# An encoder layer on one core: the output projection and the gate as plain products with pre-split A sides

## The chip, the core and the metric

One core of a Trainium2 chip runs the whole program once. The engines are TensorE (PE, with its weight loads as PEld), VectorE (DVE), ScalarE (ACT), GpSimd (POOL) and SyncE (SP), which issues the transfers between DRAM and SBUF. The metric is the device time of one execution in microseconds, from the first to the last instruction and what lies around that; lower is better.

## What is computed

A hybrid encoder layer on two sequences of 1024 tokens of width 1024, a prompt and a sample, in float32. The part that the change touches, cut from the reference:

```python
att = attention_mixer(q, k, v, rel_bias)
ssm = ssm_mixer(u, ..., w_glu, b_glu)
mix = jnp.concatenate([rms_norm(att, g_att_out), rms_norm(ssm, g_ssm_out)], axis=-1)
h = h + mix @ w_out
f = rms_norm(h, g_mlp)
h = h + jnp.square(jax.nn.relu(f @ w_mlp1)) @ w_mlp2
e = rms_norm(h, g_ple)
h = h + jax.nn.sigmoid(e @ w_ple_gate) * (p_i @ w_ple_proj)
return rms_norm(h, g_final)
```

`w_out` and `w_ple_gate` are 1024x1024, `w_mlp1` is 1024x4096, `w_ple_proj` 256x1024. The mixers' outputs `att` and `ssm` are 512 wide each.

## The kernel before

**Split precision.** Every float32 operand of a matmul is split into a high part (`hi`, a cast on ACT, L1145) and a low part (`lo`, the operand less `hi`, on DVE or POOL, L1146). `mm3` multiplies hi by hi, lo by hi and hi by lo into one PSUM bank, so one product step is three matmuls, at L451, L452 and L453. A matmul here has a 128x128 stationary side and a 128x512 moving side.

**Three phases.** Phase A norms the input, projects q, k, v and u and runs the state-space mixer. Phase B runs the dilated attention of both sequences, with the GLU of the mixer (`Glu`, its norm at L1035) and the norm of the attention's output (`att_norm`) woven in. Its order is written by hand: tasks of generators that name the engine and the place at which they go on. Phase C (`PhaseC.run`) goes through the sequences one after the other: `mix @ w_out` into `h`, the MLP in 8 chunks of 512 hidden columns, the gate, the final norm. In phase C the program text is put in order by a scheduler that simulates a timeline; each engine then works in that fixed order, and so does SP with its transfers.

**The mixers' outputs.** `Glu` (sequence by sequence) and `att_norm` (prompt in phase B) or `AttNorm` (sample, one token tile or two per chunk of the prompt's MLP) store transposed float32 tiles in the DRAM scratch `ssm` and `mixa`. Phase C loads them as `mix0mixa`, `mix0ssm` (tokens 0 to 511, L1210) and `mix1mixa`, `mix1ssm` (512 to 1023).

**The products.** `product` multiplies A (features x tokens) and B (weights, a half of 512 columns) over k steps of 128. In each step it splits A's 128x512 piece on ACT and DVE and B's on ACT and POOL, from the pool `ops` with three buffers of each kind, and issues 12 matmuls into four PSUM banks of the pool `pm2` (five banks). `strassen` forms a 2x2 block product from seven such block products. For `w_out` and the gate a block product has four k steps, 48 matmuls. Its sums of blocks are operations of 128x1024 or 128x2048 on DVE and POOL (L1174 to L1185), before which the next block product cannot be split. `into_h` and, in the gate, `read` add the banks into `u2`, `h`, `g2`, `g22` and `pre`. The MLP's second product uses `strassen` in chunks 0 to 6 and plain `product` in chunk 7.

**Around them.** The norm of `h` (`norm`, one call for each half of four token tiles) takes squares on ACT, a Newton iteration on DVE, a scaling (`ft`, L524), transposes on PE (`n_ps`, L529) and `put`: for the MLP into `Act`, high and low part; for the gate into `Blocks`, float32, split later in `product`. In the gate `pj` is `p @ w_ple_proj` for one token tile and half, 6 matmuls into a bank of `pm1` (three banks), and `sg` (L1381, L1382, from the pool `raw` with three tiles) the sigmoid and its product with `pj`.

## Time and profile before

| | us |
|---|---|
| median of 3 runs | 2838.79 |
| fastest and slowest of them | 2838.08, 2844.15 |
| the profiled execution | 2836.98 |
| its span, first to last instruction | 2835.2 |
| PE busy | 2583.4 (91%), 12014 matmuls |
| DVE busy | 1888.1 (67%) |
| ACT, POOL busy | 1177.9, 1231.5 |

The profile is of one execution; the times of single instructions are from it. Matmuls overlap in the engine, so the mean duration of one (about 0.4 us) is longer than the distance between two that follow each other. "Idle before" in a row is time in which the engine stood still ahead of those instructions, and the name behind the arrow is what ended it.

### The profile page before, as it was taken

What the parts mean: (1) busy time and instruction counts of PE and PEld (TensorE: products, weight loads), DVE (VectorE), ACT (ScalarE), POOL (GpSimd) and SP (SyncE); (2) the same over time, 40 slices, a digit from 0 to 9 for tenths busy, and PEclk for the clock granted to TensorE, in tenths of its full rate; (3) what the DMA queues carried; (4) which work ended last, traced back from release to release, by engine and by line L of the source; (5) the groups of instructions that cost most, each with busy time, mean ns of one, the idle gap of its engine ahead of it and who ended that gap; (6) DMA issues with size and microseconds to landing.
All of it is one profiled execution on the core that took longest, in us unless ns stands there. A gap on an engine that the chain in (4) does not pass through costs nothing.

```text
span 2835.2 us, 33802 instructions
## 1 busy us (share of the span) xinstructions
PE 2583.4 (91%) x12014; PEld 2036.4 (72%) x12014; DVE 1888.1 (67%) x3075; ACT 1177.9 (42%) x2370; POOL 1231.5 (43%) x845
## 2 busy tenths in 40 slices
PE   6998888969998789999999998968899999999986
PEld 5766766755566567888888776746788888888765
DVE  7867786566777784555765638799555555447677
ACT  5323323336568244333333335434433333333534
POOL 2122333223322553544645536565444555545554
PEclk9989988989999899999999999989999999999998
DMA  9524543354444401211221022142011111111201
GB/s 326 130 56 120 163 155 105 94 172 141 125 144 158 160 30 41 67 53 56 67 64 52 23 90 71 53 155 101 30 53 52 45 41 56 60 56 43 84 8 60
DMA packets 252264, 252.46 MB, mean 89 GB/s; under 512 B 41136, under 2 KB 208048, under 8 KB 250048
## 3 DMA queue, kind: packets, MB, share of 16 engines
q1 hardware_dynamic: 251072, 250.18, 27.8%
q8 instruction: 94, 1.54, 0.2%
q14 instruction: 74, 0.61, 0.1%
q0 software_dynamic: 1024, 0.13, 0.0%
HBM read 188.76 MB, written 59.27 MB: 87 GB/s over the span
## 4 chain that ended last, share of the span: by engine, by line
PE 66%; DVE 24%; issue 4%; DMA 3%; ACT 3%; POOL 1%; SPq 0%; DVEq 0%; ACTq 0%; POOLq 0%
PE m L452 16%; PE m L451 16%; PE m L453 16%; DVE lo L1146 3%; DVE h L1231 2%; PE ag L453 2%; PE glu L992 2%; PE ag L451 2%; PE ag L452 2%; PE pss L761 1%; PE po L822 1%; PE pt L801 1%; PE n_ps L529 1%; PE s_pb L251 1%; DVE s_br L358 1%
## 5 line engine op out<-in xcount | busy, mean ns | idle before, releaser
L452 PE MATMUL m<-hi,lo 128*128 128x512 f32 x1360 | 535.7, 403 | 61.4 <-DVE lo L1146 60.8
L1146 POOL TENSOR_TENSOR lo<-wr_b,hi 128x512 fp32r<-128x512 f32 x228 | 334.1, 1475 | 512.3 <-ACT hi L1145 487.3
L453 PE MATMUL m<-lo,hi 128*128 128x512 f32 x1360 | 528.3, 400 | 1.1 <-POOL lo L1146 1.0
L451 PE MATMUL m<-hi 128*128 128x512 f32 x1360 | 499.6, 402 | 19.6 <-DVE h L1231 8.6
L1231 DVE TENSOR_TENSOR h<-h,m 128x512 f32<-128x512 f32 x512 | 326.6, 678 | 139.8 <-PE m L453 139.8
L451 PE MATMUL m<-acth,hi 128*128 128x512 f32 x1024 | 400.2, 392 | 5.1 <-DVE actl L447 4.1
L453 PE MATMUL m<-actl,hi 128*128 128x512 f32 x1024 | 400.1, 391 | 3.6 <-DVE actl L447 3.6
L452 PE MATMUL m<-acth,lo 128*128 128x512 f32 x1024 | 400.1, 391 | 0.0
L452 PEld LDWEIGHTS m<-hi,lo 128*128 128x128 f32 x1360 | 262.7, 194 | 131.4 <-DVE lo L1146 76.1
L451 PEld LDWEIGHTS m<-hi 128*128 128x128 f32 x1360 | 260.9, 193 | 82.1 <-DVE h L1231 13.6
L453 PEld LDWEIGHTS m<-lo,hi 128*128 128x128 f32 x1360 | 262.9, 193 | 58.9 <-POOL lo L1146 2.4
L1145 ACT CAST hi<-wr_b 128x512 fp32r<-128x512 f32 x228 | 141.4, 621 | 377.6 <-PE m L452 339.7
L1146 DVE TENSOR_TENSOR lo<-hid,hi 128x512 fp32r<-128x512 f32 x200 | 183.6, 920 | 160.9 <-ACT hi L1145 160.9
L1146 POOL TENSOR_TENSOR lo<-w,hi 128x512 fp32r<-128x512 f32 x128 | 178.1, 1399 | 149.3 <-ACT hi L1145 136.5
L451 PEld LDWEIGHTS m<-acth,hi 128*128 128x128 f32 x1024 | 192.2, 188 | 49.1 <-ACT acth L446 5.1
L453 PEld LDWEIGHTS m<-actl,hi 128*128 128x128 f32 x1024 | 192.6, 188 | 46.2 <-DVE actl L447 4.9
L452 PEld LDWEIGHTS m<-acth,lo 128*128 128x128 f32 x1024 | 192.7, 188 | 41.2
L1293 ACT ACTIVATE hid<-m 128x512 f32<-128x512 f32 x128 | 76.1, 595 | 222.5 <-PE m L453 222.4
L453 PE MATMUL ag<-actl,whi 128*128 128x512 f32 x384 | 153.1, 400 | 0.0
L451 PE MATMUL ag<-acth,whi 128*128 128x512 f32 x384 | 152.8, 398 | 0.0
L452 PE MATMUL ag<-acth,wlo 128*128 128x512 f32 x384 | 152.6, 397 | 0.0
L1145 ACT CAST hi<-hid 128x512 fp32r<-128x512 f32 x200 | 123.3, 618 | 33.7 <-DVE hid L1181 32.1
(382 smaller groups left out, 4692.5 us busy)
## 6 DMA issues: line engine op xcount, KB each, us to landing
w<-in_w_mlp_dram SPq DMA_DIRECT2D x128, 256.0 KB, 2.8
wr_b<-in_w_mlp_dram SPq DMA_DIRECT2D x32, 1024.0 KB, 4.9
wraw<-in_w_in_dram SPq DMA_DIRECT2D x32, 512.0 KB, 4.4
out_dram<-h SPq DMA_DIRECT2D x16, 512.0 KB, 2.7
v<-zv SPq DMA_DIRECT2D x8, 576.0 KB, 6.5
xt<-in_x_sample_dram SPq DMA_DIRECT2D x8, 512.0 KB, 8.1
xt<-in_x_prompt_dram SPq DMA_DIRECT2D x8, 512.0 KB, 5.9
act_scr<-acth SPq DMA_DIRECT2D x4, 1024.0 KB, 7.3
```

The source lines that it names most:

```text
L251: nc.tensor.matmul(pb[:, k], w[:, i, g + k], u[:, g + k], start=True, stop=True)
L358: v.tensor_tensor(q4(sre), q4(sre), S_, op=ALU.mult)
L451: nc.tensor.matmul(out, l[0], r[0], start=first, stop=False)
L452: nc.tensor.matmul(out, l[1], r[0], start=False, stop=False)
L453: nc.tensor.matmul(out, l[0], r[1], start=False, stop=last)
L529: nc.tensor.transpose(pt[:, i], dst[:, P * k:P * k + P], ident)
L761: self.nc.tensor.matmul(pss[h][:, u, w], ql, kr, start=True, stop=True)
L992: nc.tensor.matmul(o, self.w[:, k, P * f:P * f + P], gt[k][:, c], start=k == 0, stop=k == 3)
L1145: self.nc.scalar.copy(hi, src)
L1146: lo_eng.tensor_tensor(lo, src, hi.bitcast(F32), op=ALU.subtract)
L1231: eng.tensor_tensor(o, o, x, op=ALU.add)
L1293: nc.scalar.activation(z, o, AF.Relu)
```

## The change

The products of `w_out` and of the gate are no longer made by `strassen` but as four plain calls of `product`, one for each half of the tokens and half of the columns, over all eight k steps: 96 matmuls each. `product` takes an `Act` as its A side and then splits only B. The A sides come split: `Glu`, `att_norm` and `AttNorm` make the high and low part and store both, in scratch of twice the size (the diff shows `att_norm`; `AttNorm.put` does the same with two tiles of its pool), and the gate's norm writes into an `Act` in place of `Blocks`, which is gone. `mixed` loads the parts into an `Act`. The pool of activation tiles is two pools of four, one for each half of the tokens; the first is opened at the end of phase B. The weights of one use are four tiles of 1 MB (`square`) in the tags of the hidden layer's and the MLP weights' tiles; `w_ple_proj`'s parts move to other tags. All adds of the gate into `h` are on DVE. The final norm goes over pairs of token tiles.

```diff
@@ class Glu
             v.scalar_tensor_tensor(go[f], go[f], self.cols[:, 4 + f:5 + f], rows, op0=ALU.mult, op1=ALU.mult)
-            nc.sync.dma_start(out=self.scr["ssm", s][f, :, 512 * th:512 * th + 512], in_=go[f])
+            hi, lo = (self.two.tile([P, 512], F32R, tag="g" + x, name="g" + x) for x in "hl")
+            nc.scalar.copy(hi, go[f])
+            nc.gpsimd.tensor_tensor(lo, go[f], hi.bitcast(F32), op=ALU.subtract)
+            for i, x in enumerate((hi, lo)):
+                nc.sync.dma_start(out=self.scr["ssm", s][i, f, :, 512 * th:512 * th + 512], in_=x.bitcast(F32))
...
@@ def att_norm
-        o = pool.tile([P, 4, P], F32, tag="ao", name="ato", bufs=2)
-        nc.scalar.copy(o, px)
+        hi, lo = (pool.tile([P, 4, P], F32R, tag="a" + x, name="ato", bufs=n) for x, n in (("h", 2), ("l", 1)))
+        nc.scalar.copy(hi, px)
+        nc.vector.tensor_tensor(lo, px, hi.bitcast(F32), op=ALU.subtract)
         B.give()
-        nc.sync.dma_start(out=scr["mixa", s][:, :, P * T:P * T + P].rearrange("f p c -> p f c"), in_=o)
+        for i, x in enumerate((hi, lo)):
+            nc.sync.dma_start(out=scr["mixa", s][i, :, :, P * T:P * T + P].rearrange("f p c -> p f c"), in_=x.bitcast(F32))
...
@@ def product
         for k in range(nk):
-            ah, al = self.split(self.ops, ("ah", "al"), a[k], [512], nc.vector)
+            if isinstance(a, Act):
+                ah, al = a.rhs(k, a.th)
+            else:
+                ah, al = self.split(self.ops, ("ah", "al"), a[k], [512], nc.vector)
             bh, bl = self.split(self.ops, ("bh", "bl"), b[k], [512], nc.gpsimd)
...
+    def mixed(cls, nc, pools, scr, s, th):
+        A = Act(pools, (th,))
+        for kq, nm in enumerate(("mixa", "ssm")):
+            for i, d in enumerate((A.hi, A.lo)):
+                nc.sync.dma_start(out=d[kq, th].bitcast(F32),
+                                  in_=scr[nm, s][i, :, :, 512 * th:512 * th + 512].rearrange("f p c -> p f c"))
+        A.th = th
+        return A
+    def square(cls, nc, bp, w):
+        u = [cls.rows(nc, w, 256 * m, bp, ("a0", "a1", "b0", "b1")[m]) for m in range(4)]
+        return [[x[l] for x in u] for l in range(2)]
...
@@ def run
-        self.strassen(A, s1, B, t2, self.into_h(h, u2, True, True, lambda: self.norm(h, gb, fa, 0)))
+        for i in range(2):
+            if i:
+                A = self.mixed(nc, self.actp, scr, s, 1)
+            for l in range(2):
+                banks = self.product(A, W[l])
+                for t in range(4):
+                    o = h[4 * i + t][:, 512 * l:512 * l + 512]
+                    v.tensor_tensor(o, o, banks[t], op=ALU.add)
+            if i == 0:
+                self.norm(h, gb, fa, 0)
...
@@ def run
-        self.strassen(e.b, self.extra("a0"), gB, gt2, read, ((0, 1), (2, 3)))
+        W = self.square(nc, self.bp, io["w_ple_gate"])
+        for i in range(2):
+            e.th = i
+            for l in range(2):
+                c = slice(512 * l, 512 * l + 512)
+                banks = self.product(e, W[l])
+                for t in range(4):
+                    T = 4 * i + t
+                    o2 = pm1.tile([P, 512], F32, tag="m1", name="pj")
+                    for k in range(2):
+                        hi, lo = pa[i, k]
+                        mm3(nc, o2, (hi[:, P * t:P * t + P], lo[:, P * t:P * t + P]), (wph[:, k, c], wpl[l][:, k]), k == 0, k == 1)
+                    sg = self.raw.tile([P, 512], F32, tag="raw", name="sg")
+                    nc.scalar.activation(sg, banks[t], AF.Sigmoid)
+                    v.tensor_tensor(sg, sg, o2, op=ALU.mult)
+                    v.tensor_tensor(h[T][:, c], h[T][:, c], sg, op=ALU.add)
```

DVE's order in the prompt's gate. `blk` is a block of the gate's A side, `m` a PSUM bank of a product, `sg` and `pre` the gate's values, `h` the residual. Before:

```order
2111 L1397 TENSOR_TENSOR pre<-g_14321,m_14736 128x512
2112 L1146 TENSOR_TENSOR lo<-blk_14234,hi 128x512
2113 L1382 TENSOR_TENSOR sg<-sg,pj 128x512 x2
2114 L1397 TENSOR_TENSOR pre<-g_14321,m_14737 128x512
2115 L1382 TENSOR_TENSOR sg<-sg,pj 128x512
2116 L1397 TENSOR_TENSOR pre<-g_14321,m_14738 128x512
2117 L1382 TENSOR_TENSOR sg<-sg,pj 128x512
2118 L1146 TENSOR_TENSOR lo<-blk_14234,hi 128x512
2119 L1146 TENSOR_TENSOR lo<-blk_14235,hi 128x512
```

and after, from the last `put` of the gate's norm:

```order
2054 L447 TENSOR_TENSOR actl_14265<-n_ps,acth_14264 128x4x128
2055 L447 TENSOR_TENSOR actl_14263<-n_ps,acth_14262 128x4x128
2056 L447 TENSOR_TENSOR actl_14265<-n_ps,acth_14264 128x4x128
2057 L1373 TENSOR_TENSOR sg<-sg,pj 128x512
2058 L1374 TENSOR_TENSOR h_8048<-h_8048,sg 128x512
2059 L1373 TENSOR_TENSOR sg<-sg,pj 128x512
```

The low parts of the A side, which stood between the gate's other work, are gone; the norm's own low parts (`actl`) stand ahead of all `sg`, and each `sg` product is followed by its add.

ACT's order at the end of phase B and the start of the first `w_out`. `sb`, `pT`, `ota` and `otb` are the attention's, `ato` is the normed attention, `wr_a` and `wr_b` are pieces of `w_out`, `w` of `w_mlp1`. Before, in the middle of the attention's last tiles:

```order
544 L832 COPY otb<-po 128x256
545 L1091 COPY ato<-n_ps 128x512
546 L793 ACTIVATE sb,sta<-sb,sta 128x256 x4
547 L805 COPY pT<-pt 128x512
548 L1145 CAST hi<-mix0mixa 128x512 x3
549 L832 COPY otb<-po 128x256
550 L1091 COPY ato<-n_ps 128x512
551 L793 ACTIVATE sb,sta<-sb,sta 128x256 x4
```

and after, behind the attention's last copy:

```order
588 L805 COPY pT<-pt 128x512
589 L832 COPY otb<-po 128x256 x2
590 L1140 CAST hi<-wr_a_7792 128x512 x2
591 L1140 CAST hi<-wr_a_7794 128x512
592 L889 ACTIVATE ea<-ea 128x16
593 L890 ACTIVATE eb<-eb 128x16
594 L1140 CAST hi<-wr_a_7794 128x512
595 L1140 CAST hi<-wr_b_7796 128x512 x2
596 L1140 CAST hi<-wr_b_7798 128x512 x2
597 L1140 CAST hi<-w_8715 128x512
598 L1140 CAST hi<-w_8721 128x512
599 L1140 CAST hi<-w_8727 128x512
```

The casts of the A side between attention steps are gone, and those of the weights start behind the attention; behind the first product's casts come four of `w_mlp1`, three of them shown, with the second product's first ones.

SP's order there. `att` is the attention's scratch of a sequence, written by `L927`; `act..` are the split A sides. Before:

```order
335 L927 DMA att_93<-at 128x8x128
336 L725 DMA vc<-zv_92 128x2x128 x4
337 L1093 DMA mixa_74<-ato 128x4x128 x4
338 L1210 DMA mix0mixa<-mixa_74 128x4x512
339 L927 DMA att_93<-at 128x8x128
340 L1093 DMA mixa_74<-ato 128x4x128 x4
341 L1132 DMA gbc<-in_g_mlp_dram 128x1024
342 L1282 DMA w_8712<-in_w_mlp_dram 128x4x128
343 L1282 DMA w_8718<-in_w_mlp_dram 128x4x128
344 L927 DMA att_93<-at 128x8x128
345 L1282 DMA w_8724<-in_w_mlp_dram 128x4x128
346 L1195 DMA wr_act<-in_w_out_dram 128x2x1024 x2
```

and after:

```order
342 L927 DMA att_93<-at 128x8x128
343 L725 DMA vc<-zv_92 128x2x128 x4
344 L1102 DMA mixa_74<-ato 128x4x128 x8
345 L1204 DMA acth_7800<-mixa_74 128x4x512
346 L1204 DMA actl_7801<-mixa_74 128x4x512
347 L1204 DMA acth_7802<-ssm_75 128x4x512
348 L927 DMA att_93<-at 128x8x128
349 L1204 DMA actl_7803<-ssm_75 128x4x512
350 L1102 DMA mixa_74<-ato 128x4x128 x8
351 L1204 DMA acth_8432<-mixa_74 128x4x512
352 L1204 DMA actl_8433<-mixa_74 128x4x512
353 L1204 DMA acth_8434<-ssm_75 128x4x512
```

Both halves of the A side are now loaded ahead of the last two stores of `att`; the loads of `w_mlp1` that stood among them follow behind the loads of `h`.

## Rows read from the trace of the kernel before

**Rows 1.** The page: busy time of each engine; shares of the last chain.

```profile
PE 2583.4 (91%) x12014; PEld 2036.4 (72%) x12014; DVE 1888.1 (67%) x3075; ACT 1177.9 (42%) x2370; POOL 1231.5 (43%) x845
...
PE 66%; DVE 24%; issue 4%; DMA 3%; ACT 3%; POOL 1%; SPq 0%; DVEq 0%; ACTq 0%; POOLq 0%
```

**Rows 2.** Windows, PE full: length, busy (count) PE/PEld/DVE/ACT/POOL, clock, DMA share, GB/s.

```profile
2575.00:2600.00 25.00, 25.00 (x111) 20.37 (x110) 22.93 (x29) 10.23 (x19) 18.51 (x14) 1.00 0.27 81
```

**Rows 3.** Windows: the three stretches that the change rewrites.

```profile
923.60:1067.70 144.10, 114.32 (x473) 89.63 (x472) 116.60 (x138) 58.48 (x105) 82.39 (x47) 0.89 0.27 93
1744.50:2026.10 281.60, 226.56 (x940) 177.27 (x938) 248.38 (x294) 124.51 (x225) 165.23 (x97) 0.91 0.24 83
2685.60:2835.20 149.60, 112.59 (x467) 89.80 (x465) 120.44 (x159) 62.34 (x113) 73.18 (x46) 0.89 0.10 38
```

**Rows 4.** Line groups, PE, 923.6–1067.7: count, busy us, mean ns, idle before, releaser.

```profile
L452 PE MATMUL m<-hi,lo 128*128 128x512 f32 x120 | 49.4, 432 | 18.1 <-DVE lo L1146 18.1
...
L529 PE MATMUL n_ps<-ident,ft 128*128 128x128 f32 x64 | 9.3, 293 | 1.4 <-DVE ft L524 1.2 <-DVE actl L447 0.2
L451 PE MATMUL m<-acth,hi 128*128 128x512 f32 x16 | 6.4, 399 | 0.0
```

**Rows 5.** Line groups, PE, 1744.5–2026.1.

```profile
L452 PE MATMUL m<-hi,lo 128*128 128x512 f32 x232 | 92.7, 421 | 30.2 <-DVE lo L1146 30.2
...
L451 PE MATMUL pj<-wph,pa 128*128 128x512 f32 x32 | 14.6, 457 | 9.2 <-DVE sg L1382 9.2
L529 PE MATMUL n_ps<-ident,ft 128*128 128x128 f32 x99 | 13.8, 286 | 4.4 <-DVE ft L524 4.0 <-DVE actl L447 0.4
```

**Rows 6.** Line groups, PE, 2685.6 to the end.

```profile
L452 PE MATMUL m<-hi,lo 128*128 128x512 f32 x112 | 44.0, 415 | 8.9 <-DVE lo L1146 8.9
...
L451 PE MATMUL pj<-wph,pa 128*128 128x512 f32 x32 | 13.9, 434 | 7.1 <-DVE sg L1382 7.1
```

**Rows 7.** Line groups, DVE, 1744.5–2026.1.

```profile
L1146 DVE TENSOR_TENSOR lo<-blk,hi 128x512 fp32r<-128x512 f32 x28 | 34.8, 1256 | 7.9 <-ACT hi L1145 7.8
...
L447 DVE TENSOR_TENSOR actl<-n_ps,acth 128x512 fp32r<-128x512 f32 x15 | 9.6, 679 | 0.7 <-ACT acth L446 0.7
...
L1383 DVE TENSOR_TENSOR h<-h,sg 128x512 f32<-128x512 f32 x4 | 7.7, 1920 | 0.0
```

**Rows 8.** Timeline, PE, first gate: start, duration, instruction, idle before, releaser.

```profile
1744.20 0.60 PE L529 MATMUL n_ps<-ident,ft 128*128 128x128 f32 x4
1744.55 0.71 PE L451 MATMUL m<-hi 128*128 128x512 f32 x2
...
1760.17 2.08 PE L452 MATMUL m<-hi,lo 128*128 128x512 f32 x4 [5.80 <-DVE lo L1146]
```

**Rows 9.** The page's DMA issues: count, KB each, median us to landing.

```profile
wr_b<-in_w_mlp_dram SPq DMA_DIRECT2D x32, 1024.0 KB, 4.9
```

**Rows 10.** The page's line groups: POOL's part of a weight split.

```profile
L1146 POOL TENSOR_TENSOR lo<-wr_b,hi 128x512 fp32r<-128x512 f32 x228 | 334.1, 1475 | 512.3 <-ACT hi L1145 487.3
```

**Rows 11.** Windows: ten microseconds at the start of the first `w_out`.

```profile
930.00:940.00 10.00, 10.00 (x36) 7.97 (x36) 5.04 (x4) 2.28 (x4) 8.13 (x5) 0.77 1.07 374
```

**Rows 12.** Timeline, DVE, end of phase B.

```profile
927.31 0.69 DVE L922 TENSOR_TENSOR at<-px,ea 128x512 f32<-128x512 f32 x1 [4.14 <-DMA att<-at]
```

**Rows 13.** Timeline, PE: last matmul of the first `w_out`; first hidden of half 1.

```profile
1040.97 0.63 PE L453 MATMUL m<-lo,hi 128*128 128x512 f32 x1
...
1067.74 0.47 PE L451 MATMUL m<-acth,hi 128*128 128x512 f32 x1 [2.06 <-DVE actl L447]
```

**Rows 14.** Timeline, PE: the kernel's last matmul.

```profile
2818.39 0.40 PE L453 MATMUL pj<-wpl,pa 128*128 128x512 f32 x1
```

**Rows 15.** Line groups, ACT, end of phase B, 780–925.

```profile
L1091 ACT COPY ato<-n_ps 128x512 f32<-128x512 f32 x8 | 4.7, 593 | 1.3 <-PE n_ps L1088 1.3
...
L1145 ACT CAST hi<-mix0mixa 128x512 fp32r<-128x512 f32 x3 | 1.7, 614 | 2.1 <-DMA mix0mixa<-mixa 2.1
```

**Rows 16.** Line groups, POOL, 780–925.

```profile
L999 POOL TENSOR_TENSOR sq<-o 128x512 f32<-128x512 f32 x4 | 4.5, 1135 | 19.1 <-PE ssq L1014 13.0 <-DVE o L998 5.1 <-DVE ga L409 1.0
```

More of the change, by code (lines that the diff above doesn't have):

```diff
@@ L1254, in run @@
         pm1 = self.pm1
[L1257 to L1262 removed]
+        A, W = first or self.first(nc, self.bp, self.actp[0], io, scr, s)
         h = []
@@ L1385, in read @@
-        def read(i, banks):
-            for t in banks:
-                if i == 1:
-                    nc.scalar.copy(g2[:, t], banks[t])
-                elif i == 6:
-                    v.tensor_tensor(g2[:, t], g2[:, t], banks[t], op=ALU.add)
-                elif i == 5:
-                    v.tensor_tensor(g22[:, t], g2[:, t], banks[t], op=ALU.add)
-                elif i == 7:
-                    v.tensor_tensor(g2[:, t], g2[:, t], banks[t], op=ALU.add)
-                if i in (2, 3, 7, 4):
-                    pre = self.raw.tile([P, 512], F32, tag="raw", name="pre")
-                    v.tensor_tensor(pre, (g2 if i in (2, 4) else g22)[:, t], banks[t], op=ALU.add)
-                    gated(i, t if i in (2, 3) else 4 + t, 0 if i in (2, 4) else 1, pre)
-            if i == 7:
-                final(range(4))
-            if i == 4:
-                final([4 + t for t in banks])
```

115 lines of the change are left out of this document (38 added, 77 removed).

## The prediction

> **What bounds the kernel now.** I read the page's shares first: PE is busy for 91% of the span and holds 66% of the chain, DVE 24% [rows 1]. So PE sets the pace over most of the program, but not everywhere, and the question is where. Next come the windows. Where PE is full, 111 matmuls take 25.00 us at clock 1.00, even where DVE is busy for 22.93 of the 25 us [rows 2]; one 512-wide matmul then costs 25 / 111 = 0.2252 us. That is the MLP. The three stretches that the change rewrites look otherwise [rows 3]: there DVE is the busiest engine (116.6 of 144.1 us, 248.4 of 281.6, 120.4 of 149.6), PE is not full, and the clock stands at 0.89 to 0.91. The line groups say who is waited for: `lo` of L1146 on DVE, that is the A side's low part, ends 18.1, 30.2 and 8.9 us of PE's idle time, and the gate's `sg` product 9.2 and 7.1 [rows 4 to 6].
>
> **How much these stretches hold.** I price PE's work in each at the full pace and look at what is left. A group of four transposes goes by in 1744.55 - 1744.20 = 0.35 us [rows 8], 0.0875 each.
> First `w_out`, 923.6 to 1067.7: 120 x 3 + 16 x 3 = 408 matmuls are 91.9, 64 transposes 5.6; of 144.1 us 46.6 are left over [rows 3, 4].
> First gate and second `w_out`, 1744.5 to 2026.1: 232 x 3 + 32 x 3 + 48 of the hidden layer (as above) = 840 are 189.2, 99 transposes 8.7; of 281.6 us 83.7 are left [rows 3, 5].
> Second gate, 2685.6 to the last matmul at 2818.8 [rows 14]: 112 x 3 + 96 = 432 are 97.3, some 36 transposes 3.1; of 133.2 us 32.8 are left [rows 6].
> Together 163 us are idle time or half clock. That is the most that any rewriting of the A sides could win here.
>
> **What the change adds on PE.** Each use goes from 7 block products of 48 matmuls to 4 products of 96: 384 for 336. With four uses that is 192 more, at 0.2252 each: 10.8, 21.6 and 10.8 us in the three stretches, 43.2 in all. This is certain and on the path.
>
> **What it takes off DVE.** In the middle stretch alone `lo<-blk` is 28 x 1.256 = 34.8 us [rows 7]; the low parts of the `w_out` sides and the Strassen sums of 128x1024 and 128x2048 go as well. What comes back is `actl` in the gate's norm, 0.68 each from PSUM [rows 7], and `h` adds that POOL did before. I estimate from these rows that DVE there goes from 88% busy to under 70%. The rest of a product's feed is the weight's split: a cast of 0.61 us on ACT [rows 15] and a subtraction of 1.475 on POOL [rows 10], against a step of 12 matmuls, 12 x 0.2252 = 2.70 us. Neither can be the limit if nothing stands ahead of it in its queue, and `ops` holds three steps.
>
> **What stays.** I go through the waits that the new order keeps or makes.
> At the start of the first `w_out` PE waits for phase B's last tiles: DVE stood 4.1 us for a store of `at` [rows 12]. The store now leaves before the `h` loads and has nothing large ahead of it, so this may go; I keep 5. PE then ran 36 matmuls in 10 us at clock 0.77 [rows 11] where 44 fit: 8 x 0.2252 = 1.8, kept as 2. The MLP norm of half 1 follows the last product: 1041.6 to 1067.7 is 26.1 us [rows 13], of which 72 matmuls and 32 transposes fill 16.2 + 2.8; 7 are kept. On ACT the casts of the first `w1` blocks stand between those of two products and wait for a load that now comes after `h`; 1, between 0 and 3. Sum 15: recovered 46.6 - 15 = 31.6, less 10.8, gives **-21**.
> In each gate the piece of the weight that goes into the tag of `hid1` can be loaded only after the last A split of chunk 7. A load of 1 MB lands after 4.9 us [rows 9] and its split takes 2.1 more, while PE has 24 matmuls, 5.4 us, ahead of needing it: between 0 and 7, taken as 3. The norm of half 1 inside the gate 2, between 0 and 5. The `pj` banks and the three `raw` tiles of `sg`, 9.2 and 7.1 before [rows 5, 6], 3 each, since `sg` no longer waits behind `lo` on DVE. The middle stretch keeps 3 + 2 + 3 + 7 (its own norm before the MLP) = 15: 83.7 - 15 - 21.6 gives **-47**. The last one keeps 8: 32.8 - 8 - 10.8 gives **-14**.
>
> **Outside the stretches.** Phase B gains casts, subtractions and stores. `att_norm` puts 8 subtractions from PSUM of 0.68, as `actl` [rows 7], on DVE, 5.4; ACT loses `hi<-mix0mixa` and the wait of 2.1 before it [rows 15], during which the attention's own work stood behind it. The GLU adds 16 casts of 0.61, 9.8, and 16 POOL subtractions, nearest L999 at 1.135 [rows 16], 18.2. At worst all is on the path, 33.4; at best the removed wait makes it -4. POOL has long waits there [rows 16] and ACT short ones [rows 15], so most of it should fit between, and I take +2. In the MLP of the first sequence each chunk's attention norm now takes three `raw` tiles instead of two, which the `w1` loads share; the weights run ahead by two blocks of 48 matmuls, 10.8 us, so I take +1, between 0 and 16 (eight times 2). The end after the last matmul, 16.4 us now [rows 3, 14], loses one `pre` and gets two interleaved final norms: +1, between -2 and +3.
> Doubled stores and loads, about 16 MB, go to stretches with DMA share 0.1 to 0.27 [rows 3], except the first `w_out`, whose half-0 loads start once half the attention is normed, ahead of need.
>
> **The sum.** -21 - 47 - 14 + 2 + 1 + 1 = -78. The profiled execution took 2836.98 us (span 2835.2 and 1.8 around it), 1.8 under the median 2838.79; 2838.8 - 78 = **2761 us**. All kept waits at their low ends (some 15 us less) and phase B at -4 instead of +2 give 2740.
>
> **Rivals.**
> *ACT becomes the gate of the products.* Casts of W stand in one in-order queue with the norms' squares, the sigmoids and, at the first `w_out`, the `w1` casts, each of which waits for someone else. If each of the 16 products loses one step of 2.70 us to that, 43 come back: **2804**. For it: the order of ACT shown with the change. Against: three steps of buffers, and a product asks ACT for only 8 x 0.61 = 4.9 us in its 21.6.
> *Phase B is stretched.* If all of the added work there lies on the path, 33.4 instead of 2: **2792**. For it: the order is made by hand, and an `h` add on DVE, both inputs in SBUF, beside POOL's splits took 1.920 where the form of that size that reads PSUM took 0.679 [rows 7], so 16 new POOL operations may slow DVE too. Against: POOL waits there longer than it works, 19.1 us before 4 operations [rows 16]. The Trainium skill, SBUF — State Buffer, "Who interferes with whom", says that a DVE operation with two SBUF inputs and a GpSimd operation that reads SBUF block each other in full; rows 7 agree, and by the rule the POOL part would cost DVE up to its own 18.2, which lies inside the 33.4.
> *PE is the bound in these stretches too.* Then the waits for `lo` only give way to others (the weights' splits, the norms), and 43.2 us of matmuls are paid: up to **2882**, slower. It decides the sign once less than 43.2 of the 163 us, 27%, is recovered. For it: PE is the busiest engine over the span at 91% [rows 1]; against: its idle time has DVE's name on it [rows 4 to 6], and dense stretches with full DVE ran at full pace [rows 2]. The Trainium skill, Perfetto Trace Analysis, "Identifying the Most-Contended Engine", would have the engine of the highest occupancy relieved first, which speaks against a change that loads it; the same section holds that TensorE's busy share doesn't tell its headroom, and rows 3 bear out the second: 79% busy there against 68% at the full pace.
> *Gain and loss cancel,* at about 2839.
>
> **How the numbers follow.** Forecast 0.64, ACT 0.15, phase B 0.10, PE-bound 0.08, no change 0.03. A run can tell about 0.2%, 5.7 us, from no change. Forecast, ACT and phase B are faster: 0.89; slower 0.08; same 0.03. The range goes from 2740 to 2812, which takes in the ACT case with some 8 us over it and leaves out the slower one and tails of the others, under 0.2.
>
> **What would show it.** In the profile after: `m` of `w_out` and gate as 128 x 3 per use with idle under 10 us, no A-side `lo` on L1140 for them; the first stretch near 123 us, the middle one near 235, the last gate near 119 to its last matmul; clock above 0.95 in each. Wrong would be: idle of PE at each product's second or third step with ACT or POOL as the releaser (ACT case), a first product later than 930 (phase B), or stretches that hold their old length with PE busy.

## The result and the profile after

| | before | after |
|---|---|---|
| median of 4 runs each, us | 2839.57 | 2788.97 |
| fastest and slowest | 2838.08, 2844.15 | 2787.51, 2794.42 |
| the profiled execution, its span | 2836.98, 2835.2 | 2789.87, 2788.1 |

The ratio of the times is 0.982, with a 95% interval from 0.981 to 0.984: 50.6 us are gone, where 78 were forecast. The time lies in the range and on the side that was forecast.

The spans can be cut at the same places of both programs: the last transpose of phase B, the first hidden-layer product of half 1 behind the norm, the start and end of the gates. All in us, the cuts read to about half a microsecond:

| stage | before | after | difference | forecast |
|---|---|---|---|---|
| to the end of phase B | 923.6 | 947.7 | +24.1 | +2 |
| first `w_out` and the norm behind it | 144.1 | 128.4 | -15.7 | -21 |
| MLP of the prompt | 676.8 | 681.8 | +5.0 | +1, both MLPs |
| first gate, second `w_out`, its norm | 281.6 | 239.8 | -41.8 | -47 |
| MLP of the sample | 659.5 | 660.2 | +0.7 | |
| second gate, to its last matmul | 133.2 | 115.8 | -17.4 | -14 |
| the end | 16.4 | 14.4 | -2.0 | +1 |
| sum | | | -47.1 | -78 |

The stretches gained 75 of the 82 us that they were to gain. Phase B took 22 more than it was given, the MLPs 5; the end gave 3 back.

First the page of the profile of the kernel after: the busy time of each engine, and the shares of the chain that ended last; it answers to [rows 1].

```profile
PE 2611.4 (94%) x12206; PEld 2058.3 (74%) x12206; DVE 1656.7 (59%) x2915; ACT 1121.8 (40%) x2258; POOL 1136.7 (41%) x817
...
PE 76%; DVE 15%; DMA 3%; issue 3%; ACT 2%; POOL 1%; SPq 0%; DVEq 0%; POOLq 0%; ACTq 0%
```

PE is busy for 94% of a shorter span instead of 91%, and its share of the chain went from 66% to 76%; that of DVE fell from 24% to 15%. Next the windows of the stretches, as [rows 3] show them: length, busy time and count of PE, PEld, DVE, ACT, POOL, the granted clock, the DMA share and GB/s.

```profile
947.70:1076.10 128.40, 117.23 (x522) 94.41 (x521) 54.05 (x88) 46.03 (x81) 64.34 (x45) 0.95 0.21 70
1757.90:1997.70 239.80, 231.49 (x1042) 187.86 (x1040) 126.03 (x201) 94.01 (x163) 108.50 (x75) 0.98 0.33 115
2657.90:2788.10 130.20, 115.80 (x523) 94.37 (x521) 66.09 (x129) 45.68 (x80) 40.40 (x30) 0.96 0.11 44
```

DVE, the busiest engine of these stretches before, is at 54.05 of 128.40, 126.03 of 239.80 and 66.09 of 130.20 us. The clock went from 0.89, 0.91, 0.89 to 0.95, 0.98, 0.96. Now who is waited for: line groups of PE in the three stretches (count, busy us and mean ns, idle time before them and its releaser), one fence for each, for [rows 4 to 6].

```profile
L451 PE MATMUL m<-hi,acth 128*128 128x512 f32 x128 | 51.4, 402 | 5.1 <-issue 5.1
L452 PE MATMUL m<-hi,actl 128*128 128x512 f32 x128 | 51.2, 400 | 0.0
L453 PE MATMUL m<-lo,acth 128*128 128x512 f32 x128 | 48.1, 400 | 0.3 <-POOL lo L1141 0.3
L529 PE MATMUL n_ps<-ident,ft 128*128 128x128 f32 x64 | 9.4, 295 | 5.8 <-DVE actl L447 5.5 <-DVE ft L524 0.2
```

```profile
L451 PE MATMUL m<-hi,acth 128*128 128x512 f32 x256 | 101.2, 396 | 2.4 <-DVE h L1269 2.4
...
L529 PE MATMUL n_ps<-ident,ft 128*128 128x128 f32 x104 | 14.6, 286 | 5.8 <-DVE actl L447 5.5 <-DVE ft L524 0.2
L451 PE MATMUL pj<-wph,pa 128*128 128x512 f32 x32 | 12.7, 395 | 0.0
```

```profile
L452 PE MATMUL m<-hi,actl 128*128 128x512 f32 x128 | 50.3, 393 | 0.0
L451 PE MATMUL m<-hi,acth 128*128 128x512 f32 x128 | 50.3, 394 | 0.0
...
L451 PE MATMUL pj<-wph,pa 128*128 128x512 f32 x32 | 12.6, 395 | 0.0
```

The waits for `lo` of 18.1, 30.2 and 8.9 us are gone, and so are those of `pj` for `sg`, 9.2 and 7.1. No wait of that size took their place: what is left is the start (5.1), the norm ahead of the MLP (5.8 in each of two stretches) and 2.4 once. The first product, in the timeline of PE (start, duration, instruction, idle before and its releaser), in the kernel before and in the one after, for [rows 11, 12]:

```profile
928.65 0.80 PE L451 MATMUL m<-hi 128*128 128x512 f32 x1 [5.02 <-DVE tb L922]
```

```profile
952.82 0.76 PE L451 MATMUL m<-hi,acth 128*128 128x512 f32 x1 [5.09 <-issue]
```

About the same 5 us, but for different reasons. In the kernel before, the product follows DVE's last `tb`, the merging of two partial attentions, which stood behind the 4.14 us for the store of `at` [rows 12]. In the kernel after that wait is down to 0.12 us, and DVE is late for another one, 3.40 us for the small load `sx`; timeline of DVE there:

```profile
947.43 0.54 DVE L885 TENSOR_TENSOR m<-sta,sx 128x16 f32<-128x16 f32 x1 [3.40 <-DMA sx<-stb]
...
952.04 0.68 DVE L922 TENSOR_TENSOR tb<-px,eb 128x512 f32<-128x512 f32 x1
```

The product starts 0.1 us behind the end of `tb` in both kernels. The profile names no releaser in the second, but in all 14 kernels run here the distance is 0.05 to 0.10 us. The small loads landed within 1.6 us before and took 4.8 to 5.0 after.

On DVE, in the middle stretch, for [rows 7]:

```profile
L447 DVE TENSOR_TENSOR actl<-n_ps,acth 128x512 fp32r<-128x512 f32 x26 | 16.8, 682 | 5.6 <-ACT acth L446 5.6
...
L1374 DVE TENSOR_TENSOR h<-h,sg 128x512 f32<-128x512 f32 x16 | 11.7, 734 | 0.5
L1373 DVE TENSOR_TENSOR sg<-sg,pj 128x512 f32<-128x512 f32 x16 | 11.0, 688 | 47.7 <-PE pj L453 47.6
```

`lo<-blk` with its 34.8 us is no longer there. The `h` adds, all 16 now on DVE, took 734 ns each in the mean, where the four in [rows 7] took 1920.

Then the one stage that grew. The timeline of ACT and of DVE in phase B, at three places where the attention falls behind that of the kernel before:

```profile
748.59 0.62 ACT L1037 CAST gh<-o 128x512 fp32r<-128x512 f32 x1 [3.86 <-DMA ssm<-gh]
```

```profile
862.08 0.63 ACT L1084 ACTIVATE junk<-att 128x512 bf16<-128x512 f32 x1 [3.20 <-DMA att<-att]
```

```profile
919.78 0.69 DVE L1099 TENSOR_TENSOR ato<-n_ps,ato 128x512 fp32r<-128x512 f32 x1 [12.57 <-DMA mixa<-ato]
```

By the starts of the same matmuls of PE, the kernel after is 1.9 us behind at the start of the attention, 6.0 behind the first place, 13.5 behind the second (4.8 of them came there, and nearly all of these are made up by 870 us), and 24.1 behind the third. ACT stood 3.86 us for the store of an earlier `gh`, and 3.20 us for the load of an attention output that `att_norm` reads; DVE stood 12.57 us for the store of the `ato` before: `att_norm` has one tile for its low part, and the next low part can't be written until that has left. The timeline of SP shows why the store was late:

```profile
901.48 0.36 SPq L1204 DMA_DIRECT2D acth<-mixa  x1
902.36 0.36 SPq L1204 DMA_DIRECT2D actl<-mixa  x1
902.77 0.50 SPq L1204 DMA_DIRECT2D acth<-ssm  x1
903.32 0.56 SPq L927 DMA_DIRECT2D att<-at  x1
903.92 5.39 SPq L1204 DMA_DIRECT2D actl<-ssm  x1
909.36 11.50 SPq L1102 DMA_DIRECT2D mixa<-ato  x4
```

and so does the chain of waits in that stretch (start, duration, what):

```profile
910.44 0.88 SPq L1102
911.36 8.30 DMA mixa<-ato
```

Four loads of 1 MB each, half 0 of the A side, are issued from 901.48 on; the issue of the last takes 5.39 us, the stores begin at 909.36, and the one that DVE waits for needs 8.30 us to land, where the page gives 2.4 as the median of that form.

### The profile page after: what moved, and what is told of

It is laid out like the page before. It is cut to its first block, busy times and chain, and to the rows that moved or that the text cites. A ratio compares the mean times of both kernels' runs of the same rounds, so it can differ in the third digit from the quotient of the medians.

```text
span 2788.1 us, 33935 instructions
## 1 busy us (share of the span) xinstructions
PE 2611.4 (94%) x12206; PEld 2058.3 (74%) x12206; DVE 1656.7 (59%) x2915; ACT 1121.8 (40%) x2258; POOL 1136.7 (41%) x817
## 4 chain that ended last, share of the span: by engine, by line
PE 76%; DVE 15%; DMA 3%; issue 3%; ACT 2%; POOL 1%; SPq 0%; DVEq 0%; POOLq 0%; ACTq 0%
PE m L453 19%; PE m L451 19%; PE m L452 19%; PE glu L992 2%; PE ag L453 2%; PE ag L451 2%; PE ag L452 2%; PE n_ps L529 1%; PE po L822 1%; PE pss L761 1%; PE pt L801 1%; DMA w<-in_w_mlp_dram 1%; PE s_pb L251 1%; PE s_py L382 1%; DVE s_br L358 1%
## 5 line engine op out<-in xcount | busy, mean ns | idle before, releaser
L1141 POOL TENSOR_TENSOR lo<-wr_b,hi 128x512 fp32r<-128x512 f32 x264 | 381.4, 1452 | 567.7 <-ACT hi L1140 544.8
L452 PE MATMUL m<-hi,lo 128*128 128x512 f32 x912 | 356.2, 393 | 3.7 <-DVE lo L1141 3.7
L453 PE MATMUL m<-lo,hi 128*128 128x512 f32 x912 | 354.2, 394 | 0.6 <-POOL lo L1141 0.6
L451 PE MATMUL m<-hi 128*128 128x512 f32 x912 | 337.6, 396 | 4.6 <-DVE h L1227 3.4
L451 PE MATMUL m<-hi,acth 128*128 128x512 f32 x512 | 202.9, 397 | 7.5 <-issue 5.1
L451 PEld LDWEIGHTS m<-hi 128*128 128x128 f32 x912 | 171.7, 189 | 44.8 <-DVE h L1227 7.1
L452 PEld LDWEIGHTS m<-hi,lo 128*128 128x128 f32 x912 | 172.3, 189 | 43.5 <-DVE lo L1141 6.8
L452 PE MATMUL m<-hi,actl 128*128 128x512 f32 x512 | 202.7, 396 | 0.0
L453 PEld LDWEIGHTS m<-lo,hi 128*128 128x128 f32 x912 | 172.2, 189 | 38.7 <-POOL lo L1141 2.1
L453 PE MATMUL m<-lo,acth 128*128 128x512 f32 x512 | 193.2, 397 | 0.3 <-POOL lo L1141 0.3
```

What stands on the lines that cost most here:

```text
L451: nc.tensor.matmul(out, l[0], r[0], start=first, stop=False)
L452: nc.tensor.matmul(out, l[1], r[0], start=False, stop=False)
L453: nc.tensor.matmul(out, l[0], r[1], start=False, stop=last)
L1141: lo_eng.tensor_tensor(lo, src, hi.bitcast(F32), op=ALU.subtract)
```

## Experiments: which part carries what

**The gate alone** on the kernel before: plain products from an `Act`; `w_out` and phase B as they were.

```diff
-                e = Blocks(self.actp)
+                e = Act(self.actp, ())
...
-        self.strassen(e.b, self.extra("a0"), gB, gt2, read, ((0, 1), (2, 3)))
+        W = self.square(nc, self.bp, io["w_ple_gate"])
+        for i in range(2):
+            e.th = i
+            for l in range(2):
+                banks = self.product(e, W[l])
...
```

> The kernel before (2839 us) with the gate alone as plain products on an A side split by the norm; `w_out` stays as it was. In the changed kernel the last gate and what follows it are 19.6 us shorter than before. If each gate gains by itself, two of them give some 37 us: 2802. If the gain of the first gate is shared with the second `w_out`, whose sums follow on DVE, less of it shows: 2810 to 2818.

2797.47 us, ratio 0.987 [0.985, 0.988]: 40.0 us below the kernel before. Windows of the prompt's gate and of the second `w_out`, which is still a `strassen`:

```profile
1742.00:1866.40 124.40, 124.40 (x564) 101.02 (x563) 70.30 (x104) 50.18 (x88) 55.16 (x37) 1.00 0.35 125
1866.40:2008.20 141.80, 109.55 (x463) 85.00 (x461) 126.01 (x165) 60.42 (x109) 80.08 (x47) 0.89 0.19 63
```

and the line group of PE that waits in the second:

```profile
L452 PE MATMUL m<-hi,lo 128*128 128x512 f32 x116 | 47.1, 428 | 24.2 <-DVE lo L1146 24.2
```

In the gate PE is busy without a gap, at clock 1.00, with more matmuls; behind it, in the same run, the old form waits 24.2 us for DVE's `lo` at clock 0.89. Both forms side by side in one run: the wait belongs to the old form and goes with it. The edit takes two things off DVE at once, the low parts of the A side and the Strassen block sums. While PE waited for `lo` in the three stretches of the kernel before, 57.1 us, DVE spent 28.7 us in `lo` itself, 12.6 in block sums and most of the rest in the norm's small steps and adds; what each is worth was not separated.

**`w_out` alone**: the kernel after with the gate of before put back (`Blocks`, `strassen`).

```diff
-                e = Act(self.actp, ())
+                e = Blocks(self.actp[0])
...
-        W = self.square(nc, self.bp, io["w_ple_gate"])
+        self.strassen(e.b, self.extra("a0"), gB, gt2, read, ((0, 1), (2, 3)))
```

> The changed kernel with the gate made as in the kernel before, by block sums on a float32 A side; `w_out` and phase B as changed. g1_gate_only took 40.0 us off the kernel before, the whole change 50.6. If the two parts add up, this one takes 10.6 off: 2828. If they share a gain in the stretch of the first gate and the second `w_out`, each alone is worth more or less than that by over 5 us. Phase B should end at 947 as in the changed kernel.

2825.33 us, 0.996 [0.994, 0.997]: 13.5 us below. Its two `w_out` stretches are 15.9 and 21.2 us shorter than before, and its phase B 27.2 us longer. 40.0 and 13.5 make 53.5, close to the 50.6 of both, so the two parts hardly touch each other: the gates bring most of the gain, and of what `w_out` wins phase B, which has to split its A sides, takes nearly three quarters back.

**Phase B alone**: the kernel before with the split, the copies and the doubled stores in `Glu` and `att_norm`.

```diff
...
-        o = pool.tile([P, 4, P], F32, tag="ao", name="ato", bufs=2)
-        nc.scalar.copy(o, px)
+        hi, lo = (pool.tile([P, 4, P], F32R, tag="a" + x, name="ato", bufs=n) for x, n in (("h", 2), ("l", 1)))
+        nc.scalar.copy(hi, px)
+        nc.vector.tensor_tensor(lo, px, hi.bitcast(F32), op=ALU.subtract)
...
-        nc.sync.dma_start(out=t, in_=scr[nm, s][:, :, 512 * i:512 * i + 512].rearrange("f p c -> p f c"))
+        nc.sync.dma_start(out=t, in_=scr[nm, s][0, :, :, 512 * i:512 * i + 512].rearrange("f p c -> p f c"))
```

> The kernel before (2839 us), with the splitting and the doubled stores of the GLU and of `att_norm` as in the changed kernel (the single `lo` tile too), but with its own products by block sums, which load the high part alone: the low part's share of the result is left out. So phase B has all the added operations and stores, and not the added loads. If the operations and stores are the price, phase B ends 20 us or more later and the time is about 2860. If the price is the wait of `lo` behind the added loads, only the rest is left: 8 to 14 us, about 2850.

2849.79 us, 1.005 [1.003, 1.007]: 12.3 us slower than before; phase B ended 18.8 us later in the profiled execution. So the price lies in phase B itself and not in the products. The longest wait of DVE for a store of `ato` there:

```profile
915.09 0.69 DVE L1096 TENSOR_TENSOR ato<-n_ps,ato 128x512 fp32r<-128x512 f32 x1 [1.86 <-DMA mixa<-ato]
```

1.86 us instead of 12.57: without the 4 MB of loads ahead of the stores that wait is small. The other 17 us are no store of `ato`. Two waits among them stand in the timeline of ACT, one ahead of a `gh`, behind which the attention is 6.0 us late, and one for the load of `att`, which adds some 2.5:

```profile
747.83 0.62 ACT L1037 CAST gh<-o 128x512 fp32r<-128x512 f32 x1 [4.38 <-DVE stb L785]
```

```profile
863.81 0.63 ACT L1081 ACTIVATE junk<-att 128x512 bf16<-128x512 f32 x1 [4.37 <-DMA att<-att]
```

The first is put down to DVE's `stb`; the tile is the same that waited for its store in the kernel after, and the experiment on the GLU's parts, below, decides.

## Experiments: what phase B waits for

**The low part in place** of the normed tile, and three tiles for the high part: no tile waits for the one low part any more.

```diff
-        hi, lo = (pool.tile([P, 4, P], F32R, tag="a" + x, name="ato", bufs=n) for x, n in (("h", 2), ("l", 1)))
+        hi = pool.tile([P, 4, P], F32R, tag="ah", name="ato", bufs=3)
+        lo = at.rearrange("p (f c) -> p f c", f=4).bitcast(F32R)
```

> The changed kernel (2789.0 us), with one edit in `att_norm`: the low part is written over the tile that was normed, one of eight, and the single `lo` tile is gone; three tiles of the high part. Theory A: phase B ends 24 us later than in the kernel before because each `lo` waits for the store of the one before it (12.6 us in one wait, with 4 MB of A-side loads ahead of the store in the queue), and because more is made and stored. Then this wait goes, the first `w_out` product starts 10 to 13 us earlier, at about 941, and the time is 2776 to 2779. Theory B: the delay is the amount of data that phase B now moves, and the wait of `lo` only shows it; then the attention's own loads wait in its place, and the time stays within 3 us of 2789.

2785.36 us, 0.982 [0.980, 0.984]: 52.1 below the kernel before it ran beside, against 50.6, no difference that counts. The wait did not go; it moved to the high part, now on ACT. Timeline of ACT, then of PE:

```profile
917.88 0.58 ACT L1099 CAST ato<-n_ps 128x512 fp32r<-128x512 f32 x1 [4.74 <-DMA mixa<-ato]
```

```profile
920.95 1.97 PE L801 MATMUL pt<-ident,sb 128*128 128x128 f32 x8 [4.47 <-ACT pT L805]
...
944.27 0.76 PE L451 MATMUL m<-hi,acth 128*128 128x512 f32 x1 [5.09 <-issue]
```

Phase B does end 8.5 us earlier than in the kernel after, and the first product starts at 944.27. But some 6 us of that are lost in the prompt's MLP, 687.8 us for 681.8: the order of the last chunk is another one, with an attention norm on DVE ahead of a `lo` that PE needs. Timeline of PE there:

```profile
1644.98 0.50 PE L452 MATMUL m<-hi,lo 128*128 128x512 f32 x1 [2.95 <-DVE lo L1142]
```

The kernel after has no wait over 1.6 us at that place. The granted clock of the 20 us behind it was 0.91, but it was 0.92 in 20 us there in the kernel after too; so the wait explains 2.95 us, and the other 3 stay open.

**Also the GLU's parts**: four tiles for its high part, its low part in place.

```diff
-            hi, lo = (self.two.tile([P, 512], F32R, tag="g" + x, name="g" + x) for x in "hl")
+            hi, lo = self.two.tile([P, 512], F32R, tag="gh", name="gh", bufs=4), go[f].bitcast(F32R)
```

> As e1_lo_in_place, and the GLU's low part is written over `go` as well, with four tiles of its high part in place of two. In the changed kernel ACT stood 3.9 us for the store of a high part, with the attention's copies behind it, and the attention is 4.2 us further behind after that place (742 to 753). Theory A: 3 to 5 us less than e1_lo_in_place, about 2773. Theory B: no less than e1_lo_in_place by 2 us.

2781.99 us, 0.981 [0.979, 0.982]: 3.4 below the last one. The attention at 753 us is 2.4 us behind the kernel before, where it was 6.0 behind in the kernel after: the 3.86 us of ACT were on the path and are gone. The MLP loses the same again, 687.3 us.

**The loads behind the stores**: the kernel after, with the loads of half 0 issued only after the last store of `att_norm`.

```diff
+            B.stored = nc.sync.dma_start(out=scr["mixa", s][i, :, :, P * T:P * T + P].rearrange("f p c -> p f c"), in_=x.bitcast(F32))
...
+        with hold:
+            return cls.mixed(nc, [a0, None], scr, s, 0), W
...
```

> The changed kernel (2789.0 us; single `lo` tile kept), with one difference in SP's order: the four loads of the A side's first half (4 MB) are issued behind `att_norm`'s last store instead of before its last eight. Nothing else moves. Theory A, corrected by e1_lo_in_place: each tile of `att_norm`, low or high, waits for the store of an earlier one, and 12 of the 24 us of phase B's delay come from those stores standing behind the loads. Then phase B ends where it ends in p1_phase_b_only or a little earlier, at 935 to 942 instead of 947.7, and the time is 6 to 12 us under the changed kernel, unless the loads, now later, hold up the first product. Theory B, the amount of data: phase B ends at 947 as before.

2788.52 us, 0.983 [0.981, 0.985]: as the kernel after. Phase B ends at 937.9 instead of 947.7, and yet the first product starts at 951.04 instead of 952.82. Timeline of PE, and windows around it:

```profile
951.04 0.76 PE L451 MATMUL m<-hi,acth 128*128 128x512 f32 x1 [13.15 <-issue]
```

```profile
920.00:935.00 15.00, 13.59 (x116) 9.37 (x114) 10.78 (x40) 12.13 (x40) 4.73 (x6) 1.00 1.01 354
935.00:947.00 12.00, 2.75 (x22) 1.85 (x18) 3.34 (x9) 2.40 (x6) 3.75 (x3) 0.76 1.06 376
947.00:951.00 4.00, 0.00 (x0) 0.00 (x0) 1.32 (x3) 0.00 (x0) 0.00 (x0) 0.50 0.14 43
```

The transfers keep the engines of the DMA full (share 1.01 and 1.06, 354 and 376 GB/s) until 947. The product does not wait for the loads of half 0: they were issued from 920.6 to 922.5 and had landed by 936.1. Again it starts 0.1 us behind the end of `tb`. Timeline of DVE:

```profile
949.65 0.69 DVE L922 TENSOR_TENSOR at<-px,ea 128x512 f32<-128x512 f32 x1 [8.17 <-DMA att<-at]
950.25 0.68 DVE L922 TENSOR_TENSOR tb<-px,eb 128x512 f32<-128x512 f32 x1
```

DVE stood 8.17 us for the store of an earlier `at`, issued at 937.93 behind the 8 MB of split A sides, which took 11.6 us to land. So the 12.57 us of DVE went, and a wait of the same kind came in their place: another tile, `at` for `ato`, whose store stands behind the loads.

**Everything in `att_norm` and the GLU that waits for a store mended, loads early** (this kernel also holds the 32 bytes of the next section; the lines with a minus are those of the kernel with the GLU's parts): the low parts of the attention and of the GLU in place, as above, four tiles for the attention's high part, and `junk` among them.

```diff
-    junk = pool.tile([P, 512], BF16, tag="junk", name="junk", bufs=1)
+    junk = pool.tile([P, 512], BF16, tag="ah", name="junk", bufs=4)
...
-        hi = pool.tile([P, 4, P], F32R, tag="ah", name="ato", bufs=3)
+        hi = pool.tile([P, 4, P], F32R, tag="ah", name="ato", bufs=4)
```

> As l3_all_mended (2764.9 us), but with the A side's first loads where the changed kernel has them, ahead of the last stores. In l3 phase B ended 18 us earlier than in the changed kernel, and the first product stood 12.9 us for the loads. If four tiles of the high part are enough, no tile waits for a store behind the loads, phase B ends at about 932 and the first product starts 5 us later, at 937 in place of 942.8: 2758 to 2761. If the stores' delay finds another tile to wait, about 2765.

2749.27 us, 0.970 [0.968, 0.971]: 87.6 below the kernel before, the fastest of all, and 16 below the kernel after with the 32 bytes alone (2765.49, next section). Phase B ends at 928.2, 19.5 us earlier than in the kernel after and 4.6 later than before. The first product:

```profile
936.29 0.77 PE L451 MATMUL m<-hi,acth 128*128 128x512 f32 x1 [8.04 <-issue]
```

In these 8.04 us DVE stood 2.61 for the store of `at`, which was issued behind the loads of half 1. Of the waits in phase B one is still there, ACT's for the load of `att`:

```profile
857.64 0.63 ACT L1084 ACTIVATE junk<-att 128x512 bf16<-128x512 f32 x1 [3.99 <-DMA att<-att]
```

**The same with the loads behind the stores**, and **with the second half of `w_out`'s weights behind the loads**, two orders of the same transfers:

```diff
+                    first = PhaseC.first(nc, bp, a0, io, scr, 0, tc.issue_after(z.ins if hasattr(z, "ins") else z))
```

> The changed kernel with the edits of e2_glu_in_place, four tiles of `att_norm`'s high part (the scratch of its squares among them), the loads behind the stores as in l1_loads_behind_stores, and the 32 bytes of x1_pad_32_bytes. By theory A no tile of phase B waits for a store that stands behind large loads, and phase B ends at about 933, 9 us after the kernel before: 2789 - 15 = 2774, and 2766 if the pad is worth its 8. By theory B not under 2782.

```diff
+        with tc.issue_after(A.loaded.ins if hasattr(A.loaded, "ins") else A.loaded):
+            u += [cls.rows(nc, io["w_out"], 256 * m, bp, tags[m]) for m in range(2, 4)]
```

> As e3_no_store_waits, with the second 2 MB of `w_out` loaded behind the A side's first half. In the changed kernel 4 MB of weights at 865 to 876 stand ahead of the attention's `vc` loads, and the attention falls 4 us further behind there. If that is their doing, phase B ends 2 to 4 us earlier than in e3_no_store_waits and so does the kernel; if not, the same time, or 3 us more should the weights come late for the first product's fifth step.

2764.91 us, 0.974 [0.972, 0.977], and 2756.79 us, 0.972 [0.971, 0.974]: 15.6 and 7.5 above. The first product starts at 942.85 and 942.27 after waits of 12.86 and 11.97 us, though phase B ends at 930.0 and 930.3; in these DVE stood 7.90 and 7.00 us for the store of `at`. The rest of the first one's 15.6 lies in the prompt's MLP, 682.9 us for 675.1, with again a `lo` of 2.95 in the last chunk, of which the order differs. Counted from the attention's start, phase B of the second is as long as that of the kernel with early loads, so moving the weights gained it nothing. Once nothing in `att_norm` or the GLU waits for a store, early loads cost phase B nothing that shows; late ones hold the store of `at`, and with it the first product.

## Experiments: the pace of the matmuls

In the kernel after, PE's full stretches had fewer matmuls than I had priced. The right-hand tiles of phase C start, in the built kernel, 32 bytes past a multiple of 64. So the kernel after was run **with a tile of 32 bytes ahead of them**, and nothing else:

```diff
+                    pad = ctx.enter_context(tc.tile_pool(name="Cpad", bufs=1, side="right")).tile([P, 8], F32, name="pad")
                     bp = ctx.enter_context(tc.tile_pool(name="Cb", bufs=1, reuse_waits="tile", side="right"))
```

> The changed kernel (2789.0 us) with a tile of 32 bytes at the end of memory, so that all later tiles on that side, the first half's activations among them, stand at multiples of 64 bytes; instructions and order as before. In the changed kernel the hidden layer's matmuls that read the first half's activations follow each other by 233.2 ns, and by 227.8 in the kernel before, where these tiles stood at multiples of 64; 1536 of them make 8.3 us. If the address decides, the distance falls to 228 and the time by about 8, to 2781. If it is the place in memory or something else, the distance stays at 233 and the time within 2.

2765.49 us, 0.975 [0.972, 0.977]: 23 us below the kernel after with its 0.982 [0.981, 0.984], nearly three times the 8 that were expected. Windows of 50 us in the first gate and in the sample's MLP, of the kernel after and of this one:

```profile
1815.00:1865.00 50.00, 50.00 (x217) 40.19 (x216) 24.24 (x46) 15.77 (x28) 18.57 (x14) 1.00 0.60 216
2300.00:2350.00 50.00, 50.00 (x219) 40.83 (x218) 22.44 (x33) 19.52 (x34) 26.57 (x18) 1.00 0.23 73
```

```profile
1806.00:1856.00 50.00, 50.00 (x223) 41.38 (x222) 24.15 (x46) 16.74 (x30) 20.11 (x15) 1.00 0.62 226
2300.00:2350.00 50.00, 50.00 (x222) 41.42 (x221) 20.21 (x28) 18.28 (x31) 27.51 (x17) 1.00 0.23 74
```

PE is busy for all 50 us in each, at clock 1.00, with 217 and 219 matmuls there and 223 and 222 here. By the spans some 7 of the 23 us lie in the three stretches and 16 in the MLPs. If the place itself and not the shift is what matters, **64 bytes** (a tile of `[P, 16]`) should do nothing:

> The changed kernel (2789.0 us) with a tile of 64 bytes where x1_pad_32_bytes has 32: the later tiles move as well, but stand off multiples of 64 bytes by 32 again. If the address modulo 64 decides, the time is 2787 to 2791 and the distance between matmuls on the first half's activations 233 ns. If the move alone did it, about 2766.

2786.74 us, 0.983 [0.980, 0.985], as the kernel after. And **the kernel before with 32 bytes** (its right-hand tiles start 32 bytes past a multiple of 64 as well, though not all of its activation tiles lie among them) should gain too:

> The kernel before (2839 us) with the same 32 bytes as x1_pad_32_bytes, opened at the same place: its weight pieces, split operands and scratch on that side then stand at multiples of 64 bytes. The pad took 22 us off the changed kernel. If it is worth as much here, the change and the address have nothing to do with each other: 2817. If the addresses of the split A sides in the change are what suffers, less: the matmuls before the change follow each other by 228 to 229 ns, 1 to 2 more than with the pad, so about 10 us: 2829.

2828.36 us, 0.998 [0.996, 0.999]: 8.5 us. The same window of the sample's MLP in the kernel before, in it with 32 bytes, and in the kernel after with 64:

```profile
2300.00:2350.00 50.00, 50.00 (x219) 40.81 (x218) 34.62 (x46) 16.68 (x29) 25.26 (x16) 1.00 0.13 42
```

```profile
2300.00:2350.00 50.00, 50.00 (x222) 41.41 (x221) 35.79 (x48) 17.91 (x32) 25.29 (x17) 1.00 0.15 44
```

```profile
2300.00:2350.00 50.00, 50.00 (x219) 40.83 (x218) 21.77 (x32) 19.23 (x33) 26.15 (x17) 1.00 0.23 74
```

219, 222, 219. The start address decides; its cost was in the kernel before as well, but smaller, 8.5 us against 23.

## Why the prediction was right, and where its sum was off

**What bounds it: right.** The three stretches were held up by DVE's work on the A sides, and their idle time was to be won. The gate alone with the old `w_out` behind it shows both in one run; how much of it was the low parts and how much the block sums, which go with them, was not separated. DVE in the middle stretch fell from 88% busy to 53%, below the 70% that I estimated.

**PE's 192 extra matmuls: right.** 12206 for 12014, and all were paid, but in stretches that no longer wait. The rival by which PE is the bound there did not come about: PE's idle time is 11.2 and 8.3 us in the first two stretches and none in the third up to the last matmul, and of the 163 us the 74.9 gained and the 43.2 paid make 118 that were recovered, far over the 27%. The Trainium skill, Perfetto Trace Analysis, "Identifying the Most-Contended Engine", says to optimize the engine of the highest occupancy first, and that TensorE's busy share is not what its headroom is judged by. The run agrees with the second: PE's busy share went from 91% to 94% [rows 1] with 192 matmuls more, and the time fell by 50.6 us. It agrees with the first only if that means ending PE's idle time; read as taking work off PE, as the prediction read it, it would have spoken against a change that gained.

**ACT as the gate of the products: did not happen.** It is busy for 46.03 of 128.40 and 94.01 of 239.80 us, and of PE's waits there only 0.3 us end on the weights' split.

**The three stretches: 82 forecast, 74.9 measured.** The first two were each some 5 us short, and the third was 3 better. Three terms were off: the pace, the kept waits and the clock. The pace: 0.2252 a matmul was 25 us by a count of 111 [rows 2], and such a count takes in matmuls that lie across the window's edges; and the tiles' place, which the kernel of before doesn't show, made them slower still. Moved by 32 bytes, the three stretches are 1.6, 3.7 and 1.8 us shorter; against the 226.7 ns that are left then (below), the count took 0.0015 off each of 1872 matmuls, 2.8 us. The kept waits: the start kept the 5 us that were put there, but by luck: the wait for the store of [rows 12], which they stood for, went, and the one for `sx` took its place. The norm behind the products kept 5.8 of the 7; but the gates kept almost nothing, where I had 8 in each for the weight's piece, `raw` and `pj`: in the last one PE's rows show 0.0 throughout, which is why it came out better. The clock: for the first `w_out` I kept 2 and for the middle none; at 0.95 over 128.40 us and 0.98 over 239.80 it took up to 6.4 and 4.8.

**Phase B: +2 forecast, +24.1 measured. This step failed**, and with it most of the difference. I added up how long the new operations last, bounded them at 33.4, and looked for gaps on their engines to put them in. The time did not go into operations. It went into waits for tiles: counted from where the attention starts, 1.9 us later than before (over all runs it starts between 0.2 us earlier and 4.6 later), 17.4 of 22.2 us are gone in the kernel in which no tile of `att_norm` or the GLU waits for a store. Of these about 3 were ACT's wait for `gh`, and some 14 those of `att_norm`, for the one tile of the low part and then for those of the high part, whose stores stood behind 4 MB of loads. The remaining 4.8 us are near the +2 that I took. Most of them, 3.7, come between 743 and 846 us, where the GLU's parts are made; ACT's 3.99 us for the load of `att` put the attention 5.6 behind, but all but 0.7 is made up by 870. What that load stands behind was tried only for 2 MB of weights, which changed nothing. I had written that the doubled stores and loads go to stretches with a DMA share of 0.1 to 0.27, "except the first `w_out`, whose half-0 loads start once half the attention is normed, ahead of need". The loads came ahead of need, indeed, but also ahead of stores that freed a tile of which there was only one; SP's order and the `bufs` of 2 and 1 were in the text of the change. The rival "phase B is stretched" had the place, and its sign, a first product later than 930, came true (952.82), but its mechanism, POOL and DVE at work on the path, was not the one; that its 2792 lies 3 us from the measured time is chance.

**The MLPs: +1 forecast, +5.7 measured.** With the tiles at multiples of 64 bytes the kernel after and the kernel before differ by 2.6 us in the prompt's MLP and -2.5 in the sample's. So the forecast holds in sum at equal places; the rest is the tiles' place, which costs the kernel after more than the kernel before. Between the two with 32 bytes there are 62.9 us.

**The end: +1 forecast, -2.0 measured.** Within its bounds of -2 and +3.

**The range was kept in part by luck.** Its upper end stood at 2812 to take in the ACT case, which did not come; nothing in it stood for waits on transfers, and these filled the room.

**The `h` adds.** [Rows 7] had four of them at 1920 ns, and I used that row for the rival only. After the change 16 took 734 each, with POOL busy for 108.50 of 239.80 us. The Trainium skill, SBUF — State Buffer, "Who interferes with whom", says that a DVE operation with two SBUF inputs and a GpSimd operation that reads SBUF lock each other out. The single adds agree. Before, three of the four overlapped an instruction of POOL and took 2877, 2864 and 1260 ns; the fourth met none and took 677. After, twelve of the 16 met none and took 691 to 694, and one that overlapped a `lo` of POOL by 0.85 us took 1391. So 1920 and 734 are means of two kinds of add, and differ first by how often the two engines met: a mean taken in one order does not hold for another.

## What to carry to other kernels

Price a new step not only by how long its operations last, but by when each tile that it writes comes free: count the buffers, find the store or load that frees one, and look what stands ahead of that in its queue. A transfer that was issued early "because it is ahead of need" delayed the later ones here, and the smallest pool behind it paid; moving the loads behind those stores only moved the wait to the next tile whose store stood behind them, and more buffers took it away. Low parts and block sums that one engine makes again for every product were worth doing without, with the low parts made once where the data is written, even for one seventh more matmuls: the engine that runs those had idle time with the first engine's name on it.

## What the chip showed that I had not expected

The distance between matmuls depends on where in SBUF their operands start. Worked out from the starts of consecutive matmuls of 128x512 in the sample's MLP, at clock 1.00, as means of groups: 226.7 ns in both kernels with the 32 bytes, where the right-hand tiles start at multiples of 64 bytes; 227.5 to 231.8 in the kernel after and 228.2 to 229.5 in the kernel before, where they start 32 bytes past one. It is 1 to 3%, but on a kernel that is 94% matmuls 23 us of 2789, for one unused tile of 32 bytes. The places of the tiles in the built programs tell more. In the kernel after, hidden-layer matmuls whose moving tile is 32 bytes off and whose stationary tile is at a multiple took 233.3 ns, those with both at a multiple 228.8, and those of the second product, with both 32 bytes off, 227.8; the kernel with 64 bytes has 233.0, 228.3 and 228.3. So it costs most where the two operands of a matmul are off differently. In the kernel before that stands only where one product follows another (232.6 to 232.9), which fits its smaller loss. Why it is so is open.
